# A two-layer hybrid backbone on one Trainium2 core: RWKV pair operands kept in DRAM between preparation and chain, and the state-space gate projected 256 columns at a time

## The chip, the cores and the metric

The kernel runs on one core of one Trainium2 chip. The metric is the device time of one execution in microseconds (us). The engines are TensorE (PE, with its weight loads as PEld), VectorE (DVE), ScalarE (ACT), GpSimd (POOL) and SyncE (SP), which issues nearly all DMAs. Before the change, three runs gave a median of 3539.37 us, from 3537.98 to 3549.52.

## The reference

Two layers over 512 tokens (256 context, 256 latent) of width 1024. A layer normalizes the tokens, projects them with one matrix `w_in`, and runs two branches on parts of the columns: an RWKV-7 branch (16 heads of 64, a delta-rule scan in both directions) and a state-space branch (8 groups of 4 heads, scans in both directions in chunks of 128). Both are gated, projected, summed and added to the stream; then a router sends each token to two of 32 experts. What the change touches is the RWKV scan and the gate of the state-space branch:

```python
def wkv7_scan(r, w, k, v, a, b, s0, reverse, emit):
    def step(S, inp):
        r_t, w_t, k_t, v_t, a_t, b_t = inp
        sa = jnp.einsum("bhij,bhj->bhi", S, a_t)
        S = S * w_t[:, :, None, :] + sa[..., None] * b_t[:, :, None, :] + v_t[..., None] * k_t[:, :, None, :]
        y = jnp.einsum("bhij,bhj->bhi", S, r_t) if emit else None
        return S, y
...
    y = y.reshape(bsz, -1, SSM_INNER) * jax.nn.silu(z.astype(F32))
    yg = y.reshape(bsz, -1, SSM_GROUPS, SSM_INNER // SSM_GROUPS)
    yg = yg * lax.rsqrt(jnp.mean(yg * yg, axis=-1, keepdims=True) + SSM_NORM_EPS)
```

`z` is the projection of the normalized tokens by 2048 columns of `w_in`, 256 for each group.

## The kernel before

**Stages.** A layer is one region. In the mixing stage the RWKV heads are worked in eight pairs of heads and the state-space branch in eight groups; then `merge` applies the branch projections, `route` the router, and the experts follow. Weights come as 512 KB pieces into `wst` (`load`, L760), ScalarE makes a half-precision high part `wh`, VectorE the low part `wl`, and each product is three matmuls.

**Order.** All calls of a layer are recorded first. `Recorder.schedule` (L519) then simulates the engines with costs per instruction and writes out one order for each engine, which the chip executes as it is. Each call belongs to a stream: `rw i` for pair i, `ssm i`, `gate i`, `mod n` and others; `mix_streams` (L1672) gives each stream a due time (96 us per pair and 99 us per group in layer 0, 100 and 105 us in layer 1). A tile has a tag; `SLOTS` (L209) says how many tiles of a tag may be held at once, and tiles of one tag are given out in the order of their streams' due times, unless `NEED` (L207) says otherwise. Streams whose name is `rw` or `sh` have weight and PSUM tags of their own (a leading `r`). SP's DMAs, stores and loads together, are in one such order too.

**One pair.** `rw_prep` (L1056) projects r, k and v, transposes v into SU, and calls `rw_dir` (L1152) for both directions, which makes the decays, the scaled operands X and Z, the transposed XT, and in matmuls `psg` the Gram matrices QA and AR. `rw_solve` (L1238) inverts sixteen unit-triangular 64x64 systems: QA goes through slB into slW, and 31 steps on VectorE, each a product slM and a sum into slY, give TT; `rw_merge` (L1287) joins the halves with QA. `rw_chain` (L1318) then forms `psat` (a transpose of Z's first half) and `psav` (QA times SU), multiplies both by TT (`psta`, `psua`), writes the first result over QA, and runs the seven dependent steps of the state (psH, St) and the outputs psY. `rw_out` (L1406) normalizes, adds bv, applies the gate and stores rwd. Z, SU, XT, QA, AR and TT have two slots each, one for each direction of one pair.

**One group.** `ssm_group` (L1474) projects x, B and C, convolves, and for each tile of 128 tokens (four in layer 0, two in layer 1) forms the scores and the outputs; the gate psz comes from two weight pieces z and u of 128 columns each, in 24 matmuls of 128 columns for each piece (L1570), with the tokens as the stationary operand:

```python
            for b in range(2):
                self.proj_t(pz[:, 128 * b:128 * b + 128], self.h, slice(128 * t, 128 * t + 128), Wz[b], 0, 128)
```

Of the kernel before, what the change touches and what calls it, by code (L numbers as in the profile page):

```python
# [12 lines left out]
F32 = mybir.dt.float32  # L13
F16 = mybir.dt.float16
BF16 = mybir.dt.bfloat16
# [6 lines left out]
NT = 512  # L22
# [52 lines left out]
def _unit_rows():  # L75

    h = (np.arange(128) // 16) % 2
    s = 2 * np.arange(16)[None, :] + h[:, None]
    return (s[:, :, None] == np.arange(32)).astype(np.float32)
# [27 lines left out]
_KDIM = {"in": 8, "rw": 8, "ssm0": 8, "ssm1": 8, "out0": 4, "out1": 4}  # L107
# [20 lines left out]
def pack(i):  # L128
# [7 lines left out]
    src = {"in": f["w_in"], "rw": f["w_branch_rw"], "ssm0": f["w_branch_ssm"][:, :1024],  # L136
# [72 lines left out]
SLOTS = {"R": 2, "sp": 2, "t5": 4, "y5": 3, "rt5": 5, "ot": 2, "z1": 4, "wst": 2, "wh": 2, "wl": 2, "rwst": 1, "rwh": 1, "rwl": 1, "r": 1,  # L209
# [3 lines left out]
CLASS = {"c4": 18, "c2": 40, "c1": 23, "ps": 8}  # L213
# [8 lines left out]
ENGINES = tuple(LAT)  # L222

# [34 lines left out]
class _Pool:  # L258
# [427 lines left out]
class Kernel:  # L686
# [10 lines left out]
    def setup(self):  # L697

        self.cp = self.pool("cp")
        self.dram = self.pool("dram", space=bass.MemoryType.DRAM)  # L700
        t = lambda n, s, d=F32: self.cp.tile(s, d, name=n)
        cst = self.cst = t("cst", [128, C_WA])
        self.c = lambda o, n=128: cst[:, o:o + n]
        self.ident = cst[:, C_ID:C_ID + 128]
        self.idb = t("idb", [128, 128], BF16)
        self.unit = t("unit", [128, 512], BF16)
        self.tri = t("tri", [128, 256], F16)
        self.io = t("io", [128, 256])
        self.iota, self.low = self.io[:, 0:128], self.io[:, 128:256]
# [12 lines left out]
        self.gd = self.dram.tile([128, 16, NT], F32, name="gd")  # L722
        self.ys = self.dram.tile([N_EXP * CAP[0], D], F32, name="ys")

    def constants(self):
# [4 lines left out]
        u = t([128, 512], F32, "unit32")  # L730
        nc.sync.dma_start(u, i["unit"].rearrange("p j t -> p (j t)"))
        nc.vector.tensor_copy(self.unit, u)
        nc.sync.dma_start(self.io, i["cst"][:, C_WS:C_T64F])
# [322 lines left out]
    def rw_prep(self, l, i):  # L1056
# [23 lines left out]
        vp = rp.tile([128, 64 + NT + 64], F32, name="v", bufs=2)  # L1080
        G.memset(vp[:, 0:64], 0.0)
        G.memset(vp[:, 64 + NT:], 0.0)
        v = S["v"] = vp[:, 64:64 + NT]
# [26 lines left out]
        for w0_ in (0, 4, 8):  # L1110
            pv = self.psum("t", [128, 4, 128], "psv")
            n = min(4, 9 - w0_)
            for w in range(n):
                T.transpose(pv[:, w], vp[:, 64 * (w0_ + w):64 * (w0_ + w) + 128], self.ident)
            if w0_ < 8:
                A.activation(SU[0][64:128, w0_:w0_ + 4, 0], pv[64:128, :, 0:64], AF.Copy)
            a = 0 if w0_ else 1
            A.activation(SU[0][0:64, w0_ + a - 1:w0_ + n - 1, 1], pv[0:64, a:n, 64:128], AF.Copy)
# [118 lines left out]

    def rw_solve(self, i):  # L1238
# [16 lines left out]
        G.tensor_copy(Y.rearrange("p j t -> p (j t)"), self.unit)  # L1255
# [62 lines left out]
    def rw_chain(self, l, i):  # L1318
# [14 lines left out]
        GT = wk.tile([128, 2, 8, 64], F32, name="GT", tag="slW")  # L1333
        St = wk.tile([128, 2, 8, 64], F32, name="St", tag="X")
        PH = []

        def batch(name, cs, out, lhs, rhs):

            ps = out or self.psum("g", [128, 8, 64], name)
            with nc.together():  # L1340
                for c in cs:
                    for e in E:
                        T.matmul(ps[rows[e], c], lhs(c, e), rhs(c, e), start=True, stop=True)
            return ps

        for d in range(2):
            SU = S["SU"][d]
            TT, XT, Z, AR = [S[x, d] for x in ("TT", "XT", "Z", "AR")]
            qa = S["QA", d].rearrange("p (c e) t -> p c e t", e=2)
            all8 = range(8)  # L1350
            mid = seq[d][1:7]

            ps = batch("psat", all8, None, lambda c, e: Z[rows[e], c, 0], lambda c, e: self.ident[rows[e], 64 * e:64 * e + 64])
            at = wk.tile([128, 8, 64], F32, name="at", tag="slY")
            A.activation(at, ps, AF.Copy)
            ps = batch("psav", all8, None, lambda c, e: qa[rows[1 - e], c, e], lambda c, e: SU[rows[1 - e], c, e])
            av = wk.tile([128, 8, 64], F32, name="av", tag="slB")
            V.tensor_copy(av, ps)
# [4 lines left out]
            ps = batch("psua", all8, None, lambda c, e: TT[rows[e], c], lambda c, e: av[rows[e], c])  # L1363
            A.activation(SU[rows[0], :, 0], ps[rows[0]], AF.Copy)
            V.tensor_copy(SU[rows[1], :, 1], ps[rows[1]])
            ps = batch("psgt", mid, None, lambda c, e: qa[rows[e], c, e], lambda c, e: XT[rows[e], c, 64 * e:64 * e + 64])
# [10 lines left out]
            ps = batch("psra", range(c0, 8), None, lambda c, e: qa[rows[e], c, e], lambda c, e: AR[rows[e], 2 * c + e])  # L1377
# [28 lines left out]
    def rw_out(self, l, i):  # L1406
# [12 lines left out]
        V.scalar_tensor_tensor(gw[64:96, 1], lo[64:96, 128:256], SW, gw[64:96, 1], op0=OP.mult, op1=OP.subtract)  # L1419
        y = wk.tile([128, NT], F32, tag="ot", name="gy", bufs=3)  # L1420
# [18 lines left out]
        G.tensor_tensor(y[:, :n], y[:, :n], S["bv"][:, :n], op=OP.add)  # L1439
# [34 lines left out]
    def ssm_group(self, l, g):  # L1474
# [59 lines left out]
        for t in range(t0, 4):  # L1534
# [34 lines left out]
            for b in range(2):  # L1569
                self.proj_t(pz[:, 128 * b:128 * b + 128], self.h, slice(128 * t, 128 * t + 128), Wz[b], 0, 128)  # L1570
# [101 lines left out]
    def mix_streams(self, l):  # L1672
# [50 lines left out]
    def route(self, l, X):  # L1723
# [63 lines left out]
        V.tensor_tensor(at, E1, E2, op=OP.add)  # L1787
        pp = self.psum("g", [128, nt, 32], "pspos")
        for t in range(nt):
            for u in range(t + 1):  # L1790
                T.matmul(pp[:, t], self.low if u == t else self.c(C_ONE), at[:, u], start=u == 0, stop=u == t)
# [391 lines left out]
```

## Time and profile before

| | us |
|---|---|
| median of three runs | 3539.37 |
| the profiled execution, its own time | 3538.96 |
| its span, first to last instruction | 3537.1 |
| TensorE busy | 3110.2 |
| VectorE busy | 2447.3 |
| ScalarE busy | 1705.4 |
| GpSimd busy | 769.3 |

The span divides into the head (to about 100 us), the mixing stage of layer 0 (to 1180), merge and router (to about 1400), the experts of layer 0 (to 1950), the mixing stage of layer 1 (2000 to 2905), its merge, and its experts. Busy times are shares of what an engine was occupied; for TensorE they hold the tails of matmuls that already run into one another, so that the distance between starts says more than a duration. In the views by tile, `first and last start` tell when the tile was worked on.

### The profile page before, as it was taken

How to read it: one execution, taken by the hardware profiler on the slowest of the kernel's cores; microseconds unless marked ns; L12 is line 12 of the kernel's file. 1: busy time of each engine (PE TensorE's matmuls, PEld its weight loads, DVE VectorE, ACT ScalarE, POOL GpSimd, SP SyncE). 2: the span in 40 equal slices, each digit the busy share in tenths (PEclk: the TensorE clock that was granted, in tenths of full speed). 3: DMA queues.
4: the chain of work that ended last, by engine and by line, in shares of the span. 5: the costliest groups of instructions: out<-in, count | busy, mean ns of one | idle time of the engine just before them, and what ended most of it. 6: DMA issues, size and time to landing. Idle time of an engine off the chain costs nothing. (4 is left out here: it accounts for less than half of the span.)

```text
span 3537.1 us, 86322 instructions
## 1 busy us (share of the span) xinstructions
PE 3110.2 (88%) x36050; PEld 2094.7 (59%) x36050; DVE 2447.3 (69%) x4491; ACT 1705.4 (48%) x3155; POOL 769.3 (22%) x1080
## 2 busy tenths in 40 slices
PE   7899889898998998999998778888889789899987
PEld 3566466475566457888886455666566668333332
DVE  4868868768778337999997788788988765221112
ACT  4554454454544325998886645554545434111111
POOL 1332332333232111111111133232333311000000
PEclk9999999999999997999999899999999889899998
DMA  7032231421312736999996411221212138999996
GB/s 283 28 106 73 93 118 51 151 100 43 120 57 98 276 104 222 412 401 397 396 394 249 154 63 45 74 69 50 75 61 71 53 125 299 346 399 398 399 398 243
DMA packets 241746, 662.65 MB, mean 187 GB/s; under 512 B 26688, under 2 KB 55104, under 8 KB 241344
## 3 DMA queue, kind: packets, MB, share of 16 engines
q1 hardware_dynamic: 236608, 640.22, 49.1%
q10 hardware_dynamic: 3584, 12.58, 0.9%
q8 instruction: 287, 4.70, 0.5%
q0 software_dynamic: 1152, 4.19, 0.3%
q14 instruction: 115, 0.94, 0.1%
HBM read 622.30 MB, written 34.60 MB: 186 GB/s over the span
## 5 line engine op out<-in xcount | busy, mean ns | idle before, releaser
L682 PE MATMUL mm<-h,wh 128*128 128x512 f16 (+1 forms) x2432 | 680.4, 363 | 11.0 <-ACT wh L682 11.0
L682 PEld LDWEIGHTS <-wh 128*128 128x128 f16 x3200 | 311.4, 99 | 280.7 <-issue 25.4
L682 PE MATMUL mm<-h,wl 128*128 128x512 f16 (+2 forms) x1216 | 439.0, 362 | 39.2 <-DVE wl L682 39.1
L682 DVE SCALAR_TENSOR_TENSOR ewl<-est,ewh 128x1024 f16<-128x1024 f32 x352 | 411.7, 1222 | 15.5 <-ACT ewh L682 12.4
L682 ACT ACTIVATE ewh<-est 128x1024 f16<-128x1024 f32 x384 | 382.6, 1049 | 32.4 <-PE pse L682 28.3
L682 DVE SCALAR_TENSOR_TENSOR wl<-wst,wh 128x1024 f16<-128x1024 f32 (+1 forms) x234 | 293.2, 1267 | 35.0 <-ACT wh L682 34.5
L682 PE MATMUL pse<-xg,ewh 128*128 128x96 f16 x4096 | 276.5, 206 | 2.9 <-DVE xg L682 0.8
L682 PEld LDWEIGHTS <-ewh 128*128 128x128 f16 x4096 | 265.8, 98 | 7.1
L682 PEld LDWEIGHTS <-wl 128*128 128x128 f16 (+1 forms) x1600 | 159.4, 100 | 181.4 <-DVE wl L682 47.9
L682 PE MATMUL pse<-xg,ewl 128*128 128x96 f16 x2048 | 264.0, 206 | 0.3 <-issue 0.2
L682 ACT ACTIVATE wh<-wst 128x1024 f16<-128x1024 f32 (+1 forms) x234 | 240.2, 1043 | 12.2 <-DMA wst<-in_wmix_dram 11.6
L682 PE MATMUL pse<-esh,xg 128*64 128x512 f32 x512 | 236.3, 597 | 0.0
L682 PE MATMUL pse<-est,xg 128*64 128x512 f32 x512 | 236.3, 597 | 0.0
L682 DVE SCALAR_TENSOR_TENSOR cva<-cvz,cwh,cva 128x512 f32<-128x512 f32 (+1 forms) x256 | 204.0, 797 | 0.4
L682 PEld LDWEIGHTS <-ewl 128*128 128x128 f16 x2048 | 199.4, 98 | 5.8 <-issue 4.1
L682 DVE TENSOR_TENSOR slM<-slY,slW 128x144 f32<-128x144 f32 (+22 forms) x496 | 175.0, 353 | 6.4
L682 POOL TENSOR_TENSOR ewl<-est,ewh 128x1024 f16<-128x1024 f32 x32 | 69.7, 2180 | 487.5 <-ACT ewh L682 414.6
L682 DVE SCALAR_TENSOR_TENSOR eyl<-psy,egs,eyh 128x512 f16<-128x512 f32 x32 | 24.0, 751 | 211.2 <-ACT eyh L682 211.2
L682 PEld LDWEIGHTS <-h 128*128 128x128 f16 x2496 | 150.0, 102 | 27.0 <-issue 21.1
L682 POOL TENSOR_TENSOR sht<-shz 128x512 f32<-128x512 f32 (+3 forms) x56 | 65.2, 1164 | 403.7 <-ACT shz L682 244.4
L682 PE MATMUL psz<-wh,h 128*128 128x128 f16 x1536 | 149.4, 225 | 0.0
L682 PE MATMUL psz<-wl,h 128*128 128x128 f16 x768 | 139.9, 225 | 8.3 <-DVE wl L682 8.3
(561 smaller groups left out, 7072.7 us busy)
## 6 DMA issues: line engine op xcount, KB each, us to landing
est<-in_w_dram SPq DMA_DIRECT2D x576, 512.0 KB, 7.5
wst<-in_wmix_dram SPq DMA_DIRECT2D x246, 512.0 KB, 4.7
esh<-in_w_dram SPq DMA_DIRECT2D x384, 256.0 KB, 6.6
wst<-in_wmod_dram SPq DMA_DIRECT2D x96, 512.0 KB, 6.0
ys<-ey ACTq DMA_DIRECT2D x32, 384.0 KB, 6.9
lot<-in_lora_dram SPq DMA_DIRECT2D x16, 256.0 KB, 4.8
gd<-gat SPq DMA_DIRECT2D x16, 256.0 KB, 2.0
smd<-smo SPq DMA_DIRECT2D x16, 256.0 KB, 3.4
```

The lines of the kernel that those rows point to most:

```text
L682: r = getattr(e, m)(*[real(x) for x in a], **{n: real(x) for n, x in k.items()})
```

## The change

Three things. **Pair operands in DRAM:** psat and psav move from the chain to the end of `rw_dir`, their results replace the first half of Z and the free half of SU; Z, SU, XT and AR are then stored to a DRAM tensor `sd`, and bv to another. The chain loads all four again into new tiles of the same tags; what it wrote over QA goes over Z, one copy of 128 rows by ScalarE in place of two of 64 rows by ScalarE and VectorE. Chain and output become a stream of their own, `ch i`, due 1 us after pair i+1's preparation and solve. GT gets a slot of its own. **The gate:** the pieces z and u are now the upper and the lower 512 rows of all 256 columns, and a tile's gate is 2 x 12 matmuls of 256 columns. **Constants:** the solve's start matrix Y is a memset by VectorE and a copy of 32 elements in place of a copy of 512; the zero borders of v go, with two half-width matmuls for the first and last block; the prefix-sum table `low` is loaded in `route`.

```diff
-        for n, o in (("x", X_ + 256 * i), ("y", X_ + 256 * i + 128), ("B", B_ + 128 * i), ("C", CC_ + 128 * i),
-                     ("z", Z_ + 256 * i), ("u", Z_ + 256 * i + 128)):
+        p += [(f"z{i}", "in0", r(Z_ + 256 * i, 256)), (f"u{i}", "in1", r(Z_ + 256 * i, 256))]
...
-SLOTS = {"R": 2, "sp": 2, "t5": 4, "y5": 3,
+SLOTS = {"GT": 1, "t5": 4, "y5": 3,
...
-CLASS = {"c4": 18, "c2": 40, "c1": 23, "ps": 8}
+CLASS = {"c4": 18, "c2": 41, "c1": 23, "ps": 8}
+LAG = 1
...
-            if tag in SPLIT and self.rec.stream[0] in ("rw", "sh"):
+            if tag in SPLIT and self.rec.stream[0] in ("rw", "sh", "ch"):
...
+        self.sd = self.dram.tile([128, 8, 2, 4, 1024], F32, name="sd")
+        self.sb_ = self.dram.tile([128, 8, NT], F32, name="sbv")
...
+        nc.sync.dma_start(self.sb_[:, i, :NT - o0], bv[:, :NT - o0])
         for d in range(2):
             self.rw_dir(l, i, d, S, kk, w0)
...
+        ps = self.batch("psat", lambda c, e: Z[rows[e], c, 0], lambda c, e: self.ident[rows[e], 64 * e:64 * e + 64])
+        A.activation(Z[:, :, 0], ps, AF.Copy)
+        ps = self.batch("psav", lambda c, e: QA[rows[1 - e], 2 * c + e], lambda c, e: SU[rows[1 - e], c, e])
+        A.activation(SU[rows[0], :, 0], ps[rows[0]], AF.Copy)
+        V.tensor_copy(SU[rows[1], :, 1], ps[rows[1]])
+        sd = self.sd[:, i, d]
+        nc.sync.dma_start(sd[:, 0], Z.rearrange("p c b t -> p (c b t)"))
+        nc.sync.dma_start(sd[:, 1], SU.rearrange("p c b t -> p (c b t)"))
+        nc.sync.dma_start(sd[:, 2], XT.rearrange("p c t -> p (c t)"))
+        if full:
+            nc.sync.dma_start(sd[:, 3], AR.rearrange("p c t -> p (c t)"))
+        else:
+            nc.sync.dma_start(sd[:, 3, 512:], AR[:, 8:].rearrange("p c t -> p (c t)"))
...
-        G.tensor_copy(Y.rearrange("p j t -> p (j t)"), self.unit)
+        V.memset(Y, 0.0)
+        G.tensor_copy(bass.AP(tensor=Y.tensor, offset=Y.offset, ap=[Y.ap[0], [34, 16], [1, 2]]),
+                      self.unit[:, None, :].to_broadcast([128, 16, 2]))
...
-            SU = S["SU"][d]
-            TT, XT, Z, AR = [S[x, d] for x in ("TT", "XT", "Z", "AR")]
+            TT = S["TT", d]
+            sd = self.sd[:, i, d]
+            Z = S["Z", d] = rp.tile([128, 8, 2, 64], F32, name="Z", bufs=4)
+            nc.sync.dma_start(Z.rearrange("p c b t -> p (c b t)"), sd[:, 0])
+            SU = rp.tile([128, 8, 2, 64], F32, name="SU", bufs=4)
+            nc.sync.dma_start(SU.rearrange("p c b t -> p (c b t)"), sd[:, 1])
+            XT = rp.tile([128, 8, 128], F32, name="XT", bufs=4)
+            nc.sync.dma_start(XT.rearrange("p c t -> p (c t)"), sd[:, 2])
+            AR = rp.tile([128, 16, 64], F32, name="AR", bufs=4)
+            nc.sync.dma_start(AR[:, 2 * c0:].rearrange("p c t -> p (c t)"), sd[:, 3, 128 * c0:])
-            ps = batch("psta", all8, None, lambda c, e: TT[rows[e], c], lambda c, e: at[rows[e], c])
-            A.activation(qa[rows[0], :, 0], ps[rows[0]], AF.Copy)
-            V.tensor_copy(qa[rows[1], :, 1], ps[rows[1]])
+            ps = batch("psta", lambda c, e: TT[rows[e], c], lambda c, e: Z[rows[e], c, 0])
+            A.activation(Z[:, :, 0], ps, AF.Copy)
...
+        bv = rp.tile([128, NT], F32, name="bv", bufs=2)
+        nc.sync.dma_start(bv[:, :n], self.sb_[:, i, :n])
...
-                self.proj_t(pz[:, 128 * b:128 * b + 128], self.h, slice(128 * t, 128 * t + 128), Wz[b], 0, 128)
+                self.proj_t(pz, lambda k: self.h(4 * b + k), tk, Wz[b], 0, 256, first=b == 0, last=b == 1)
...
             self.rw_solve(i)
+            rec.at(1, ("ch", i), h + 60e3 + P * (i + 1 + LAG) + 1e3)
             rec.tight = True
             self.rw_chain(l, i)
```

## Rows read from the trace of the kernel before

**Rows 1.** The page's slices: busy tenths of TensorE, VectorE, 88.4 us each.

```profile
PE   7899889898998998999998778888889789899987
...
DVE  4868868768778337999997788788988765221112
```

**Rows 2.** Stretches: length, PE, PEld, DVE, ACT, POOL busy, clock, DMA share, GB/s.

```profile
141.00:1075.00 934.00, 844.44 (x10330) 568.99 (x10328) 719.25 (x1475) 450.34 (x1008) 298.97 (x429) 0.96 0.27 93
2068.00:2822.00 754.00, 640.30 (x8138) 473.56 (x8137) 631.12 (x1336) 378.87 (x830) 251.62 (x412) 0.93 0.20 63
```

**Rows 3.** Tile slW, layers 0 and 1: count, ns min/median/max, first, last start.

```profile
L682 DVE STREAM_TRANSPOSE slW<-slB x8: 1924/1955/1974, 141.4 to 1074.5; 128x1024 f32<-128x1024 f32 x8
...
L682 DVE STREAM_TRANSPOSE slW<-slB x8: 1892/1936/1977, 2067.7 to 2821.5; 128x1024 f32<-128x1024 f32 x8
```

**Rows 4.** Stretches of one pair: solve, chain, prep; layer 0, then layer 1.

```profile
672.00:725.00 53.00, 45.30 (x287) 26.79 (x284) 50.90 (x114) 19.41 (x39) 14.07 (x25) 0.90 0.09 32
725.00:751.00 26.00, 24.14 (x688) 22.34 (x687) 14.14 (x31) 11.00 (x30) 4.72 (x6) 1.00 0.14 43
751.00:811.00 60.00, 53.24 (x510) 33.49 (x509) 41.25 (x70) 34.24 (x78) 25.07 (x32) 0.97 0.44 154
2277.00:2329.00 52.00, 43.15 (x274) 28.39 (x275) 48.36 (x113) 18.93 (x35) 15.40 (x24) 0.84 0.15 49
2329.00:2356.00 27.00, 24.86 (x654) 21.32 (x652) 20.61 (x43) 14.50 (x38) 3.21 (x7) 1.00 0.08 27
2356.00:2391.00 35.00, 26.58 (x249) 19.92 (x247) 25.29 (x42) 21.73 (x48) 16.31 (x30) 0.90 0.35 110
```

**Rows 5.** Tile Z of one pair: layer 0, then layer 1.

```profile
L682 PE MATMUL psg<-Z,X x64: 272/272/579, 792.3 to 807.6; 64*128 64x128 f32 x64
...
L682 PE MATMUL psY<-Z,St x56: 218/218/267, 751.4 to 753.0; 64*64 64x64 f32 x56
...
L682 PE MATMUL psat<-cst,Z x64: 218/218/267, 2329.7 to 2339.5; 64*64 64x64 f32 x64
...
L682 PE MATMUL psg<-Z,X x64: 272/272/579, 2372.9 to 2387.9; 64*128 64x128 f32 x64
...
L682 PE MATMUL psY<-Z,St x32: 218/218/267, 2356.5 to 2357.5; 64*64 64x64 f32 x32
```

**Rows 6.** DMA issues, us to landing; SP's waits from 141 to 1075.

```profile
wst<-in_wmix_dram SPq DMA_DIRECT2D x246, 512.0 KB, 4.7
...
smd<-smo SPq DMA_DIRECT2D x16, 256.0 KB, 3.4
...
xd<-xres SPq DMA_DIRECT2D x6, 512.0 KB, 3.0
...
SPq L682 <- PE psH L682: 231.4, 19, 58.7
```

**Rows 7.** Stretches: the fullest 100 us of the mixing stages.

```profile
300.00:400.00 100.00, 95.36 (x1361) 68.96 (x1360) 76.13 (x147) 54.50 (x130) 36.20 (x50) 1.00 0.32 104
```

**Rows 8.** Tile QA from 141 to 1075 us: the copy of psta.

```profile
L682 DVE COPY QA<-psta x14: 694/695/695, 200.8 to 1012.7; 64x512 f32<-64x512 f32 x14
```

**Rows 9.** Tile psz; its stretches; its weight loads; timeline of 512-column matmuls.

```profile
L682 PE MATMUL psz<-wh,h x32: 219/219/219, 161.2 to 163.8; 128*128 128x128 f16 x32
L682 PE MATMUL psz<-wl,h x16: 219/219/219, 161.2 to 163.8; 128*128 128x128 f16 x16
...
141.00:1075.00 934.00, 85.40 (x1344) 18.38 (x56) 0.96 0.27 93
2068.00:2822.00 754.00, 44.75 (x672) 9.43 (x28) 0.93 0.20 63
...
L682 PEld LDWEIGHTS <-h 128*128 128x128 f16 x2496 | 150.0, 102 | 27.0 <-issue 21.1
...
2289.00 0.38 PE L682 MATMUL mm<-h,wl 128*128 128x512 f16 x1
...
2290.94 0.38 PE L682 MATMUL mm<-h,wl 128*128 128x512 f16 x1
```

More of the change, by code (lines that the diff above doesn't have):

```diff
@@ L77, in _unit_rows @@
     h = (np.arange(128) // 16) % 2
-    s = 2 * np.arange(16)[None, :] + h[:, None]
-    return (s[:, :, None] == np.arange(32)).astype(np.float32)
+    return (h[:, None] == np.arange(2)).astype(np.float32)
 R_, WF_, WB_, K_, V_, AF_, AB_, G_ = 0, 1024, 1088, 1152, 2176, 3200, 3264, 3328
@@ L96, in _mix_pieces @@
     for i in range(8):
-        for n, o in (("x", X_ + 256 * i), ("y", X_ + 256 * i + 128), ("B", B_ + 128 * i), ("C", CC_ + 128 * i),
-                     ("z", Z_ + 256 * i), ("u", Z_ + 256 * i + 128)):
+        for n, o in (("x", X_ + 256 * i), ("y", X_ + 256 * i + 128), ("B", B_ + 128 * i), ("C", CC_ + 128 * i)):
             p.append((f"{n}{i}", "in", r(o, 128)))
+        p += [(f"z{i}", "in0", r(Z_ + 256 * i, 256)), (f"u{i}", "in1", r(Z_ + 256 * i, 256))]
     for j in range(8):
@@ L104, in _mix_pieces @@
     return p
-_KDIM = {"in": 8, "rw": 8, "ssm0": 8, "ssm1": 8, "out0": 4, "out1": 4}
+_KDIM = {"in": 8, "in0": 4, "in1": 4, "rw": 8, "ssm0": 8, "ssm1": 8, "out0": 4, "out1": 4}
 MIX = {}
@@ L135, in pack @@
     o["wmod"] = f["w_mod"].reshape(DEPTH, 8, 128, 3, 4, 2, 256).transpose(0, 3, 1, 5, 2, 4, 6)
-    src = {"in": f["w_in"], "rw": f["w_branch_rw"], "ssm0": f["w_branch_ssm"][:, :1024],
+    src = {"in": f["w_in"], "in0": f["w_in"][:, :512], "in1": f["w_in"][:, 512:], "rw": f["w_branch_rw"], "ssm0": f["w_branch_ssm"][:, :1024],
            "ssm1": f["w_branch_ssm"][:, 1024:], "out0": f["w_out"][:, :512], "out1": f["w_out"][:, 512:]}
@@ L208 @@
 SPLIT = {"wst", "wh", "wl", "mm", "t", "t5"}
-SLOTS = {"R": 2, "sp": 2, "t5": 4, "y5": 3, "rt5": 5, "ot": 2, "z1": 4, "wst": 2, "wh": 2, "wl": 2, "rwst": 1, "rwh": 1, "rwl": 1, "r": 1,
+SLOTS = {"GT": 1, "t5": 4, "y5": 3, "rt5": 5, "ot": 2, "z1": 4, "wst": 2, "wh": 2, "wl": 2, "rwst": 1, "rwh": 1, "rwl": 1, "r": 1,
          "k": 1, "v": 1, "kkt": 1, "bv": 1, "lot": 1, "lh": 1, "log": 1, "ll": 1, "gw": 1, "SU": 2, "Z": 2, "XT": 2, "QA": 2, "AR": 2, "TT": 2,
@@ L705, in setup @@
         self.idb = t("idb", [128, 128], BF16)
-        self.unit = t("unit", [128, 512], BF16)
+        self.unit = t("unit", [128, 2])
         self.tri = t("tri", [128, 256], F16)
-        self.io = t("io", [128, 256])
-        self.iota, self.low = self.io[:, 0:128], self.io[:, 128:256]
+        self.iota = t("iota", [128, 128])
         self.id2 = t("id2", [128, 64])
@@ L729, in constants @@
         nc.vector.tensor_tensor(self.id2, self.ident[:, 0:64], self.ident[:, 64:128], op=OP.add)
[L730 to L733, printed above, removed]
+        nc.sync.dma_start(self.unit, i["unit"])
+        nc.sync.dma_start(self.iota, i["cst"][:, C_IOTA:C_IOTA + 128])
         u = t([128, 256], F32, "tri32")
@@ L1079, in rw_prep @@
         k = S["k"] = rp.tile([128, NT], F32, name="k", bufs=2)
[L1080 to L1083, printed above, removed]
+        v = S["v"] = rp.tile([128, NT], F32, name="v", bufs=2)
         ps = self.psum("mm", [128, NT])
@@ L1109, in rw_prep @@
         S["SU"] = SU
-        for w0_ in (0, 4, 8):
+        for w0_ in (0, 4):
             pv = self.psum("t", [128, 4, 128], "psv")
[L1112 to L1116, printed above, removed]
+            with nc.together():
+                for w in range(4):
+                    if w + w0_:
+                        T.transpose(pv[:, w], v[:, 64 * (w0_ + w) - 64:64 * (w0_ + w) + 64], self.ident)
+            if not w0_:
+                with nc.together():
+                    T.matmul(pv[64:128, 0], v[:, 0:64], self.ident, start=True, stop=True)
+                    T.matmul(pv[0:64, 0], v[:, NT - 64:NT], self.ident, start=True, stop=True)
+                A.activation(SU[0][0:64, 7, 1], pv[0:64, 0, 64:128], AF.Copy)
+            A.activation(SU[0][64:128, w0_:w0_ + 4, 0], pv[64:128, :, 0:64], AF.Copy)
             a = 0 if w0_ else 1
-            A.activation(SU[0][0:64, w0_ + a - 1:w0_ + n - 1, 1], pv[0:64, a:n, 64:128], AF.Copy)
+            A.activation(SU[0][0:64, w0_ + a - 1:w0_ + 3, 1], pv[0:64, a:4, 64:128], AF.Copy)
         G.tensor_copy(SU[1][64:128, :, 0], SU[0][64:128, :, 0])
@@ L1236, in rw_dir, with batch @@
                                     mi[:, None, :].to_broadcast([128, 4, 64]), op=OP.mult)
+        rows = self.rows2
+        SU = S["SU"][d]
+        ps = self.batch("psat", lambda c, e: Z[rows[e], c, 0], lambda c, e: self.ident[rows[e], 64 * e:64 * e + 64])
[11 more added lines that the diff above has]
+            nc.sync.dma_start(sd[:, 3, 512:], AR[:, 8:].rearrange("p c t -> p (c t)"))
+    rows2 = (slice(0, 64), slice(64, 128))
+    def batch(self, name, lhs, rhs, cs=range(8)):
+        ps = self.psum("g", [128, 8, 64], name)
+        with self.nc.together():
+            for c in cs:
+                for e in range(2):
+                    self.nc.tensor.matmul(ps[self.rows2[e], c], lhs(c, e), rhs(c, e), start=True, stop=True)
+        return ps
     def rw_solve(self, i):
@@ L1332, in rw_chain @@
         yo = lambda c, e: py[rows[e], 64 * c - o0:64 * c - o0 + 64]
-        GT = wk.tile([128, 2, 8, 64], F32, name="GT", tag="slW")
+        GT = wk.tile([128, 2, 8, 64], F32, name="GT")
         St = wk.tile([128, 2, 8, 64], F32, name="St", tag="X")
         PH = []
[L1337 to L1344, printed above, removed]
@@ L1346, in rw_chain @@
-        for d in range(2):
-            SU = S["SU"][d]
-            TT, XT, Z, AR = [S[x, d] for x in ("TT", "XT", "Z", "AR")]
-            qa = S["QA", d].rearrange("p (c e) t -> p c e t", e=2)
-            all8 = range(8)
-            mid = seq[d][1:7]
[L1353 to L1358, printed above, removed]
-            ps = batch("psta", all8, None, lambda c, e: TT[rows[e], c], lambda c, e: at[rows[e], c])
-            A.activation(qa[rows[0], :, 0], ps[rows[0]], AF.Copy)
-            V.tensor_copy(qa[rows[1], :, 1], ps[rows[1]])
-            ps = batch("psua", all8, None, lambda c, e: TT[rows[e], c], lambda c, e: av[rows[e], c])
+        batch = self.batch
@@ new lines, in rw_chain @@
+        for d in range(2):
+            TT = S["TT", d]
[8 more added lines that the diff above has]
+            nc.sync.dma_start(AR[:, 2 * c0:].rearrange("p c t -> p (c t)"), sd[:, 3, 128 * c0:])
+            mid = seq[d][1:7]
+            ps = batch("psta", lambda c, e: TT[rows[e], c], lambda c, e: Z[rows[e], c, 0])
+            A.activation(Z[:, :, 0], ps, AF.Copy)
+            ps = batch("psua", lambda c, e: TT[rows[e], c], lambda c, e: SU[rows[e], c, e])
@@ L1364, in rw_chain @@
             A.activation(SU[rows[0], :, 0], ps[rows[0]], AF.Copy)
             V.tensor_copy(SU[rows[1], :, 1], ps[rows[1]])
-            ps = batch("psgt", mid, None, lambda c, e: qa[rows[e], c, e], lambda c, e: XT[rows[e], c, 64 * e:64 * e + 64])
+            ps = batch("psgt", lambda c, e: Z[rows[e], c, 0], lambda c, e: XT[rows[e], c, 64 * e:64 * e + 64], mid)
             for cs in ((slice(0, 3), slice(5, 8)) if d else (slice(1, 7),)):
@@ L1376, in rw_chain @@
                                  skip_group_check=True)
-            ps = batch("psra", range(c0, 8), None, lambda c, e: qa[rows[e], c, e], lambda c, e: AR[rows[e], 2 * c + e])
+            ps = batch("psra", lambda c, e: Z[rows[e], c, 0], lambda c, e: AR[rows[e], 2 * c + e], range(c0, 8))
             V.tensor_tensor(Z[:, c0:, 1], Z[:, c0:, 1], ps[:, c0:], op=OP.add)
@@ L1438, in rw_out @@
         A.activation(y[:, :n], y[:, :n], AF.Identity, scale=self.pv("lnw", 1, i), bias=self.pv("lnb", 1, i))
-        G.tensor_tensor(y[:, :n], y[:, :n], S["bv"][:, :n], op=OP.add)
+        G.tensor_tensor(y[:, :n], y[:, :n], bv[:, :n], op=OP.add)
         pg = self.psum("t", [128, NT], "psgate")
@@ L1787, in route @@
         V.tensor_tensor(at, E1, E2, op=OP.add)
+        low = self.tile([128, 128], F32, "low")
+        nc.sync.dma_start(low, self.i["cst"][:, C_LOW:C_LOW + 128])
         pp = self.psum("g", [128, nt, 32], "pspos")
@@ L1790, in route @@
             for u in range(t + 1):
-                T.matmul(pp[:, t], self.low if u == t else self.c(C_ONE), at[:, u], start=u == 0, stop=u == t)
+                T.matmul(pp[:, t], low if u == t else self.c(C_ONE), at[:, u], start=u == 0, stop=u == t)
         pos = tl("pos")
```

## The prediction

> **What bounds the kernel now.** I read the slices first: between the head and the expert stages lie two mixing stages (100 to 1180 us and 2000 to 2905 us, slices 2 to 13 and 24 to 32) in which TensorE's digits go from 7 to 9 and VectorE's from 6 to 9 [rows 1]. The experts' stages contain nothing that the change touches, so the question is what sets the pace of the mixing stages. The busy time over seven periods of the RWKV pairs says that no engine does: TensorE is busy 844.4 of 934 us in layer 0 and 640.3 of 754 us in layer 1, VectorE 719.3 and 631.1 us, and the DMA engines 0.27 and 0.20 of the time [rows 2]. The pairs themselves keep a strict beat: the first wide transpose of the solve (slW) comes eight times between 141.4 and 1074.5 us, and eight times between 2067.7 and 2821.5 us, which is 133.3 and 107.7 us per pair [rows 3]. The table by phase of one pair shows why [rows 4]. During the solve (52 to 53 us) VectorE is busy 0.93 to 0.96 of the time and TensorE 0.83 to 0.85; during merge and chain (26 to 27 us) it is the reverse, TensorE 0.92 to 0.93, VectorE 0.54 to 0.76; in the rest (60 us in layer 0, 35 us in layer 1), the next pair's preparation, TensorE has 0.89 and 0.76. So the three phases run one after another, each full on one engine only. The operands that hold them apart are visible by their times: the last matmul of the chain that reads Z is at 2357.5 us, and the next pair's first Gram matmul with its own Z comes at 2372.9, its last at 2387.9; in layer 0 it is 753.0, then 792.3 to 807.6 [rows 5]. Z, SU, XT, QA and AR have two buffers each (one per direction), so pair i+1 can't have its operands before the chain of pair i is done.
>
> **The change part by part.**
>
> *Parking and the lag.* Prep now ends with the transposes psat and psav, and Z, SU, XT and AR go to DRAM; their buffers come free before the solve instead of after the chain. QA stays in SBUF, but its last reader is now the merge. The chain of pair i, which reloads the four tiles, ranks behind the prep of pair i+1, and so falls beside the solve of pair i+1. The ring chain-prep-solve falls into two shorter rings:
> - Buffers: chain from the last psat on (2339.5 to 2357.5, 18 us), prep up to the last Gram matmul (807.6-751.4 = 56 us in layer 0, 2387.9-2356.5 = 31 us in layer 1 [rows 5]), psat and psav with their copies at most 10 us (with the merge they lie between 2329 and 2339.5), a store and a reload at 3.0 and 4.7 us to landing [rows 6] about 8 us: 92 and 67 us.
> - QA: solve 52 us, merge at most 10 (the same stretch), the two Gram rounds 15 (2372.9 to 2387.9), the transposes before the solve 3 (to 2391): 80 us.
>
> Both are shorter than 133.3 and 107.7 us, so the engines set the pace next. How full can they get? I take 0.94, between the 0.93 of the chains [rows 4] and the best 100 us of the stage, 95.4 [rows 7]. Layer 0: 844.4/0.94 = 898 instead of 934, gain 36 us (VectorE would allow 765). Layer 1: 640.3/0.94 = 681 instead of 754, gain 73 us (VectorE, 623/0.94 = 662, is close behind). First prep and last chain have no partner before or after, so I count seven periods of eight. Ends: at 0.98, 72 and 101 us; at half the effect, 55 us together.
>
> *Its own cost.* psat and psav are the same 128 matmuls each; they now run beside the solve's first steps, which don't wait for them. Per pair VectorE loses two copies of 0.694 us (psta now goes through ScalarE alone) [rows 8] and gains a memset of Y of 512 elements (not in the trace; between 0.1 us and that copy's 0.7; I take 0.2, since it reads nothing): 1.2 us less, which is the 623 above. ScalarE gains two such copies and is idle for half of the stage [rows 2]. POOL's copy of Y shrinks; its cover is the same solve start. Nine transposes of v become seven and two half-width matmuls: no difference. SP issues 18 DMAs more per pair, eight stores and eight loads of 512 KB (the AR ones half in layer 1) and bv twice: 8.4 MB and 7.3 MB. The DMA engines moved 93 GB/s at 0.27 busy, so 344 GB/s when full [rows 2]: 24 us more of DMA time per pair beside the 36 that it has now, in a period of 125. That is no bound. SP, however, is one queue in order: it waited 231 us for the chain's psH in layer 0, once 58.7 us [rows 6]. A store of a parked tile waits for ScalarE or VectorE, a reload for a free buffer, and behind both stand the weight loads, which have three buffers. I cost it at nothing, because a weight piece feeds about 5 us of matmuls and two more are loaded by then; without that cover it is the second rival.
>
> *The gate (psz).* 2304 matmuls of 128 columns become 1152 of 256. The columns are the same. 48 of them start between 161.2 and 163.8 us, one each 56 ns; nine of 512 columns take 1.94 us, 216 ns each, so 256 columns take 108 [rows 9]. The sum at this rate goes from 129 to 124 us. Over both layers TensorE is busy 130 us for 2016 of them, 65 ns each [rows 9], part of it tails and low clock: at most 24 us. I take 6. The Trainium skill, page "TensorE: Matmul & The Clock Gate", section "Back-to-back issue gap", gives about 81 ns for a sustained pair of weight load and 128-column matmul and 131 ns for 512; by that the edit would save an estimated 36 us or more. The rows disagree at both widths, and I go by them.
>
> *Rest.* The smaller unit constant saves a little in the head, the table for the router's prefix sum is now loaded in the router's stage, ahead of its use: nothing either way, at worst 2 x 4.7 us of landing.
>
> **Sum.** The profiled execution took 3538.96 us, 0.4 us under the median of the runs. 3539-36-73-6 = 3424; I say 3425.
>
> **The rivals.**
> 1. *The solve stays the bound.* VectorE is already 0.93 to 0.96 full there; its chain of small dependent instructions is stretched by every instruction of the chain that now comes between. If in layer 1 VectorE's idle time of 17.6 us per period ((754-631)/7) falls only to 14, and layer 0 gains 2 us a period, it is 7 x 5.6 = 39 us: 3500 (between 3490 and 3539). For it: the full solve phase. Against it: layer 0 has 31 us of idle VectorE per period.
> 2. *SP's queue (slower).* Stores that wait for their producers hold back weight loads, and TensorE starves. It decides from 115/14 = 8.2 us of starving per pair; at 12 us it is 168-115 = 53 us: 3592. For it: the long waits of SP [rows 6]. Against it: with those waits TensorE is still 0.90 busy in layer 0.
> 3. *Slow DRAM pieces (slower).* Each parked tile is 128 pieces of 4 KB, 256 KB apart. The 256 KB of smd, also spread, took 3.4 us, half a weight piece 2.4 [rows 6]. It decides at four times the time of contiguous pieces: 96 + 36 = 132 us of DMA in a period that was 133. At 4.25 times layer 0 needs 138 us and layer 1 (21 us of parking, 22 of its own) 112: 7 x 4.7 + 7 x 4.3 = 63 us more than now, less 6: 3596. Against it: smd is 1.4 times, not four. The Trainium skill, page "DMA: Bandwidth & Descriptors", section "Latency and other measured facts", says that large powers of two as the pitch of rows cost bandwidth, 207 GB/s at 512 KB and 103 at 4 MB. No run here shows it yet.
> 4. *Weight loads bound psz after all.* If each pair cost its weight load's 102 ns [rows 9], 2304 would take 235 us and half as many 124: 111 instead of 6, so 3320. The 56 ns speak against it. It is the rule of the page on TensorE named above, at its hardest.
>
> **How the numbers follow.** Forecast 0.62 (3340 to 3490), rivals 0.18, 0.12, 0.04, 0.04. About 0.3%, 11 us, is what a measurement of this kernel can tell from no change. The first rival gives 0.12 faster and 0.06 same; slower are the second and third: 0.78, 0.06, 0.16. The range 3320 to 3530 holds the forecast with its ends and most of the first rival, and leaves out the slower ones.
>
> **What would show it.** The chain's psta and psua should start while slM of the next pair runs; slW should beat every 120 to 128 and 95 to 100 us; TensorE's busy share should be near 0.94 in both layers; psz should take 108 ns per matmul. Longer solves (over 60 us) at the same beat speak for the first rival; TensorE waiting for wh or wl behind SP for the second; landings of the parked tiles over 15 us for the third. I am wrong if the beat falls and the time does not, or if it stays at 133 and 108 us.

## The result and the profile after

The changed kernel takes 3479.13 us (median of four, 3478.76 to 3486.93), the kernel before 3541.14 us in the same comparison: a ratio of 0.9827 [0.9804, 0.9849], 62 us or 1.7 % faster. I had forecast 3425 us. The execution that was profiled is the slowest of the four, 3486.93 us; its span is 3484.8 us, 52.3 us under that of before.

Tile slW of the changed kernel, layers 0 and 1, answers to [rows 3] (count, ns, first and last start):

```profile
L683 DVE STREAM_TRANSPOSE slW<-slB x8: 1908/1953/1970, 153.1 to 1039.3; 128x1024 f32<-128x1024 f32 x8
...
L683 DVE STREAM_TRANSPOSE slW<-slB x8: 1889/1944/1967, 2041.9 to 2772.1; 128x1024 f32<-128x1024 f32 x8
```

The beat is 126.6 and 104.3 us, 6.7 and 3.4 us shorter. In layer 0 that makes 47 us over seven periods, yet the layer ends only 22.7 us earlier: its first slW comes 11.7 us later, and the last one's distance to the end of the merge grew by 11 us. The stretches of those seven periods in each layer (columns of [rows 2]):

```profile
153.10:1039.30 886.20, 815.30 (x9180) 530.82 (x9177) 696.20 (x1439) 447.75 (x1005) 286.32 (x405) 0.97 0.46 164
2041.90:2772.10 730.20, 632.84 (x7471) 458.85 (x7471) 605.30 (x1306) 376.57 (x821) 246.54 (x389) 0.92 0.39 134
```

TensorE is busy 0.92 and 0.87 of them, against 0.90 and 0.85 before. It does 29 us less in layer 0's periods than in [rows 2]. Half of that work now stands ahead of the first slW, the other half in the tail behind the last one. The head up to the first slW, before (first) and after (second):

```profile
0.00:141.40 141.40, 106.72 (x779) 58.53 (x780) 86.75 (x165) 74.95 (x155) 30.16 (x51) 0.94 0.50 186
```

```profile
0.00:153.10 153.10, 121.45 (x957) 65.32 (x957) 92.94 (x175) 84.27 (x166) 35.61 (x57) 0.89 0.49 188
```

The tail, from just behind the last slW to the end of the merge's matmuls, before (first) and after (second):

```profile
1076.80:1305.20 228.40, 213.69 (x1798) 119.92 (x1797) 120.62 (x215) 73.29 (x123) 30.30 (x39) 0.96 0.45 157
```

```profile
1041.80:1281.20 239.40, 228.50 (x1972) 128.32 (x1973) 128.13 (x230) 78.69 (x135) 36.29 (x42) 0.96 0.53 185
```

TensorE fills this tail to 0.95 and has 15 us more work there, as it has in the head. One pair in three stretches as in [rows 4], but now solve, rest of the preparation, Gram rounds, since the previous pair's chain lies beside the solve; layer 0, then layer 1:

```profile
508.00:556.00 48.00, 45.01 (x739) 28.95 (x736) 44.70 (x113) 23.51 (x46) 9.44 (x17) 1.00 0.45 163
556.00:622.00 66.00, 62.65 (x529) 39.40 (x518) 43.69 (x73) 38.66 (x96) 26.72 (x34) 1.00 0.49 180
622.00:637.30 15.30, 14.83 (x198) 10.00 (x196) 13.48 (x30) 6.43 (x12) 4.44 (x11) 1.00 0.90 336
...
2336.00:2384.00 48.00, 43.92 (x649) 29.43 (x646) 46.00 (x118) 24.58 (x51) 10.24 (x21) 1.00 0.31 107
2384.00:2418.70 34.70, 33.47 (x289) 25.85 (x289) 28.63 (x51) 22.15 (x53) 18.83 (x28) 0.90 0.38 126
2418.70:2443.50 24.80, 17.90 (x307) 14.64 (x306) 18.65 (x34) 9.28 (x20) 6.84 (x11) 0.79 0.68 256
```

During the solves TensorE's share rose from 0.85 and 0.83 to 0.94 and 0.92: much of the chain moved there, as meant. The chain's psta against the steps slM of the solve, one pair of layer 1, before (first) and after (second):

```profile
L682 PE MATMUL psta<-at,TT x64: 218/218/267, 2337.0 to 2342.4; 64*64 64x64 f32 x64
...
L682 DVE TENSOR_TENSOR slM<-slY,slW x31: 155/318/1004, 2280.0 to 2328.2; 128x144 f32<-128x144 f32 x3, 128x4 f32<-128x4 f32 x2, 128x16 f32<-128x16 f32 x2, 128x36 f32<-128x36 f32 x2
```

```profile
L683 PE MATMUL psta<-Z,TT x64: 218/218/267, 2335.4 to 2357.6; 64*64 64x64 f32 x64
...
L683 DVE TENSOR_TENSOR slM<-slY,slW x31: 149/318/467, 2338.9 to 2377.6; 128x144 f32<-128x144 f32 x3, 128x4 f32<-128x4 f32 x2, 128x16 f32<-128x16 f32 x2, 128x36 f32<-128x36 f32 x2
```

Before, psta came after the last step of its own pair's solve. Now its first direction starts just ahead of the next pair's steps, its second among them. Layer 0's pair is 0.95 full over its period. Layer 1 has a hole in the Gram rounds: 0.72, at a clock of 0.79 (part of it at 1.2 GHz), with the DMA engines at 0.68. What TensorE waited for in layer 1's periods (us in total, times, longest):

```profile
PE psta L683 <- DMA Z<-sd: 17.4, 8, 3.8
PE pscw L683 <- ACT lp L683: 11.8, 5, 4.5
PE psW L683 <- DVE slO L683: 8.1, 5, 2.3
PE psua L683 <- DMA SU<-sd: 6.3, 4, 1.9
```

The first and the fourth are reloads of parked tiles. Landings of these, and of a weight piece of the same size, from the table of DMA issues (KB, median us):

```profile
wst<-in_wmix_dram SPq DMA_DIRECT2D x246, 512.0 KB, 6.3
...
sd<-XT SPq DMA_DIRECT2D x32, 512.0 KB, 3.6
sd<-Z SPq DMA_DIRECT2D x32, 512.0 KB, 4.0
sd<-SU SPq DMA_DIRECT2D x32, 512.0 KB, 4.9
XT<-sd SPq DMA_DIRECT2D x32, 512.0 KB, 5.6
Z<-sd SPq DMA_DIRECT2D x32, 512.0 KB, 6.2
SU<-sd SPq DMA_DIRECT2D x32, 512.0 KB, 7.2
```

### The profile page after: what moved, and what is told of

Its sections match the earlier page's. It is cut to its first block, busy times and chain, and to the rows that moved or that the text cites. A ratio compares the mean times of both kernels' runs of the same rounds, so it can differ in the third digit from the quotient of the medians.

```text
span 3484.8 us, 84587 instructions
## 1 busy us (share of the span) xinstructions
PE 3117.4 (89%) x34930; PEld 2072.5 (59%) x34930; DVE 2418.7 (69%) x4474; ACT 1725.3 (50%) x3189; POOL 773.3 (22%) x1048
## 5 line engine op out<-in xcount | busy, mean ns | idle before, releaser
L683 DVE TENSOR_TENSOR slM<-slY,slW 128x144 f32<-128x144 f32 (+22 forms) x496 | 162.7, 328 | 8.3
L683 ACT ACTIVATE eu<-pse 128x384 f32<-128x384 f32 (+1 forms) x64 | 34.5, 540 | 243.4 <-PE pse L683 243.4
L683 DVE TENSOR_REDUCE slY<-slM 128x2 f32<-128x4 f32 (+23 forms) x496 | 147.3, 297 | 7.2
L683 PE MATMUL psz<-wh,h 128*128 128x256 f16 x768 | 150.3, 283 | 0.0
```

What stands on the lines that cost most here:

```text
L683: r = getattr(e, m)(*[real(x) for x in a], **{n: real(x) for n, x in k.items()})
```

## The experiments

All times in one table; layer 0 is counted to the end of the last `ey` in the profiled execution, layer 1 is the rest of its span, and the beat is the mean distance of slW. The ratio is to the kernel before, from runs of the same session; that kernel's median was 3541 us beside the change and 3544 to 3546 in the later sessions, so differences to the changed kernel, which are of medians, are good to some 5 us.

| kernel | median us | ratio [95 %] | layer 0, 1 (us) | beat 0, 1 (us) |
|---|---|---|---|---|
| before | 3541.1 | 1 | 1930.6, 1606.5 | 133.3, 107.7 |
| changed | 3479.1 | 0.9827 [0.9804, 0.9849] | 1907.9, 1576.9 | 126.6, 104.3 |
| e1 parking only | 3486.6 | 0.9838 [0.9825, 0.9852] | 1922.6, 1563.5 | 129.9, 101.0 |
| e2 gate only | 3505.9 | 0.9891 [0.9874, 0.9909] | 1916.2, 1590.6 | 130.7, 105.7 |
| e3 no lag | 3535.6 | 0.9981 [0.9971, 0.9991] | 1948.6, 1585.5 | 136.3, 105.5 |
| e4 last chain due earlier | 3481.0 | 0.9822 [0.9809, 0.9835] | 1905.0, 1576.9 | 127.5, 103.9 |
| e5 gate in the old order | 3541.1 | 0.9986 [0.9975, 0.9997] | 1933.9, 1610.2 | 133.8, 107.7 |
| e6 reloads reckoned at 4.0 us | 3462.8 | 0.9764 [0.9748, 0.9780] | 1899.4, 1570.3 | 126.4, 101.5 |
| e7 half solve, before | 3433.7 | 0.9685 [0.9669, 0.9702] | 1875.4, 1556.4 | 126.3, 102.0 |
| e8 half solve, changed | 3451.2 | 0.9733 [0.9717, 0.9748] | 1907.1, 1543.3 | 129.6, 100.0 |
| e9 e6 and e4 | 3448.5 | 0.9729 [0.9715, 0.9744] | 1896.1, 1559.5 | 126.1, 101.6 |
| e10 e1 and e6 | 3484.1 | 0.9833 [0.9818, 0.9848] | 1914.7, 1567.5 | 128.1, 101.6 |
| e11 a copy before each reload | 3608.2 | 1.0177 [1.0159, 1.0194] | 1984.9, 1625.5 | 137.9, 110.3 |
| e12 another order | 3477.2 | 0.9811 [0.9788, 0.9835] | 1893.3, 1585.9 | 125.0, 104.1 |

### Which part brings it: e1 to e4

e1 puts back the six 128-column pieces and the old gate loop; e2 is the kernel before with the other side of that diff:

```diff
-                self.proj_t(pz[:, 128 * b:128 * b + 128], self.h, slice(128 * t, 128 * t + 128), Wz[b], 0, 128)
+                self.proj_t(pz, lambda k: self.h(4 * b + k), tk, Wz[b], 0, 256, first=b == 0, last=b == 1)
```

> The change with its gate part undone: z and u are projected 128 columns at a time from the old packing, the parking stays. Theory A (the parking brings the gain, by splitting the ring of a pair): 3476 to 3490 us, since the 24 gate matmuls of a tile take 109 ns each after the change where 48 took 54 ns each before; beats of slW 126 and 104 us as in the changed kernel. Rival B (the gate brings a good part): 3500 us or more, with the beats nearer to 133 and 108 us.

> The kernel before with the new gate alone, nothing parked. Theory A: 3533 to 3545 us, no change that can be measured, beats of slW 133 and 108 us. Rival B (the gate brings a good part of the 62 us): 3520 us or less.

The parking alone takes 58 us off, the gate alone 38, both together 62. e1's time came as theory A says, though not its beats, 129.9 and 101.0 us where I expected 126 and 104. e2 didn't: a part that I had put at 6 us brought 38, and the two don't add.

e3 sets `LAG = 0`; e4 changes one due time:

```diff
-            rec.at(1, ("ch", i), h + 60e3 + P * (i + 1 + LAG) + 1e3)
+            rec.at(1, ("ch", i), h + 60e3 + P * (i + 1 + LAG * (i < 7)) + 1e3)
```

> The changed kernel with the due time of each pair's chain one period earlier (LAG 0), so that parked operands come back as soon as the solve is done. Theory A (what counts is that the buffers are free, the chain may run early): 3480 to 3500 us, with the beats of slW within 2 us of 126 and 104. Rival C (what counts is that the chain is allowed to run late and fill the solve of the next pair): 3515 to 3545 us, nearly all of the gain gone, with beats near 133 and 108 us.

> The changed kernel with the last pair's chain alone due one period earlier. In the changed kernel the stretch from the last slW of layer 0 to the end of the branch took 241.9 us where it took 230.7 before, and the last chain's St took 40 us of it. Theory D (the late due time starves the last chain, and the merge waits for it): 3455 to 3470 us, 10 to 25 us less than the changed kernel, with the tail of layer 0 back under 231 us. Rival E (TensorE is busy there with work that has to be done anyway): 3473 to 3485 us, the tail unchanged in sum.

e3 is rival C: with the chain due in its own pair's period, parking and gate together give 7 us (0.9981 of 3544), less than the gate alone. That is 56 us above the changed kernel, more than an order alone moves anything below (33 us). So it isn't the empty buffers that pay but the permission to run the chain a period late, beside the next solve. The lag also lengthens the head: e3 has its first slW at 139.6 us, the changed kernel at 153.1. e4 is rival E: the last chain of layer 0 is done 33 us earlier (its last St starts at 1111.7 instead of 1145.1 us), yet the merge ends only 1.6 us earlier. In that tail TensorE is full of work that has to be done anyway, which is what the two tail rows above show.

### Why the gate alone brings 38 us: e5

The matmuls are 256 wide, but recorded and priced as two of 128, and merged only when the order is written out:

```diff
+                        for c in (0, 128):
+                            nc.tensor.matmul(pz[:, c:c + 128], zx, Wz[b][w][:, k, c:c + 128], **f)
+                        nc.wide[len(nc.ops) - 2] = [("matmul", (pz, zx, Wz[b][w][:, k, 0:256]), f)]
+                        nc.wide[len(nc.ops) - 1] = []
...
-                for m, a, k in o.calls:
+                for m, a, k in self.wide.get(i, o.calls):
```

> The kernel before with the gate's matmuls 256 columns wide from the new packing, but everything put in order as if they were still 128 wide, so that each engine's order is that of the kernel before with two narrow matmuls replaced by one wide one. The gate alone took 38 us off where nothing was expected of it. Theory F (the narrower count of matmuls changes the order in which the list scheduler puts all engines' work, and the gain is that order, with fewer matmuls falling into half clock): 3530 to 3545 us. Rival G (the width itself saves TensorE time): 3500 to 3515 us, as the gate alone with its own order.

Theory F. In the old order the wide gate is worth 5 us (0.9986 of 3546; the interval gives 1 to 9). The other 33 us belong to the order that the scheduler happened to write: ScalarE's 3155 instructions come in the same order in the traces of e5 and of the kernel before, and in another one in e2. One way in which an order pays is visible: the same matmuls, in the seven periods of each layer, e5 first, then e2:

```profile
141.20:1077.00 935.80, 845.05 (x9652) 557.33 (x9650) 718.04 (x1472) 449.94 (x1007) 300.21 (x429) 0.96 0.27 92
2070.90:2825.00 754.10, 637.60 (x7802) 464.16 (x7801) 630.97 (x1337) 378.35 (x830) 251.54 (x412) 0.93 0.20 63
```

```profile
141.90:1056.80 914.90, 834.47 (x9653) 549.13 (x9651) 710.92 (x1473) 449.33 (x1007) 297.61 (x429) 0.98 0.28 94
2054.40:2794.20 739.80, 625.96 (x7799) 452.75 (x7798) 621.45 (x1334) 377.06 (x830) 254.25 (x412) 0.95 0.20 64
```

An equal number of matmuls (within 3) occupies TensorE 10.6 and 11.6 us less, at a granted clock that is 0.02 higher: less of it fell to 1.2 GHz. The stretches are 21 and 14 us shorter, so the clock goes with about two thirds of it; whether it causes the shorter stretch or follows from fewer pauses isn't settled by these rows.

The gate's own matmuls run as forecast. One gate of the changed kernel, 24 matmuls of 256 columns:

```profile
L683 PE MATMUL psz<-wh,h x16: 272/273/273, 2398.1 to 2400.6; 128*128 128x256 f16 x16
L683 PE MATMUL psz<-wl,h x8: 272/273/273, 2398.2 to 2400.5; 128*128 128x256 f16 x8
```

### Is the solve still the bound: e7 and e8

`for t in range(16, 32)` becomes `range(16, 17)`: steps 17 to 31 of the solve are left out, in the kernel before and in the changed one.

> The kernel before with steps 17 to 31 of the solve left out, so 30 of its 62 VectorE instructions per pair are gone and its last inverse rows are not computed. Theory A (the ring prep, solve, chain sets the pace before the change): each layer falls until TensorE's 0.94 is the bound, 35 us in layer 0 and 70 us in layer 1, so 3420 to 3470 us. Rival (the ring is not the bound): 3525 us or more.

> The changed kernel with steps 17 to 31 of the solve left out, as in the run before this one. Theory A (parking has taken the solve off the path): 0 to 20 us less than the changed kernel, 3459 to 3479 us. Rival 1 of the prediction (the solve still bounds through the buffers that it holds or through VectorE): 40 us less or more, 3439 us or less, as much as the same cut saves in the kernel before.

The cut saves 112 us before the change (0.9685 of 3546), as theory A says, though by layer it is 55 and 50 us and not 35 and 70. After it, 28 us, between theory A and rival 1, and by layer it is both: layer 0 is the same within 1 us (1907.1 for 1907.9), layer 1 falls by 34 us (1543.3 for 1576.9). Of these, 16 us lie below every order here with the whole solve (the best is e9's 1559.5). The seven periods with half a solve, kernel before first, then changed:

```profile
141.90:1026.00 884.10, 832.29 (x10336) 566.65 (x10336) 649.91 (x1265) 454.01 (x1015) 300.92 (x429) 0.98 0.28 98
2012.50:2726.60 714.10, 630.41 (x8115) 471.10 (x8114) 558.48 (x1123) 379.71 (x828) 249.73 (x412) 0.94 0.21 66
```

```profile
149.20:1056.60 907.40, 828.99 (x9211) 540.53 (x9207) 644.16 (x1232) 444.98 (x1006) 287.56 (x409) 0.95 0.45 161
2041.40:2741.30 699.90, 613.20 (x7489) 446.47 (x7489) 547.91 (x1099) 375.10 (x821) 250.67 (x395) 0.94 0.41 141
```

Without parking and with half a solve TensorE reaches 0.941 in layer 0, the 0.94 that I had taken, but only 0.883 in layer 1; with both it is 0.876 there. And once the solve is short, the changed kernel is the slower of the two, 3451 for 3434 us: parking with the new gate then costs 17 us. All of it and more lies in layer 0, which takes 1907.1 us with parking and 1875.4 without.

### What the reloads cost: e6, e9, e10, e11, e12

e6 gives the scheduler a truer landing time for the reloads, e10 the same on e1, e9 e6 with the diff of e4:

```diff
         o.lat = 900 if o.bytes and eng == "scalar" else 1500 if o.bytes and eng != "sync" else LAT[eng]
+        if o.bytes and eng == "sync" and reads[0].tensor.name.startswith("sd"):
+            o.lat = 4000
```

> The changed kernel with the scheduler told that a reload of a parked tile lands 4.0 us after its transfer instead of 0.9 us, so that reloads are issued earlier or their readers put later; nothing else is changed. In the changed kernel TensorE waits 17.4 us for Z and 6.3 us for SU in the beats of layer 1, 3.8 and 6.1 us in layer 0. Theory H (these waits and what queues behind them are why layer 1 gained 24 us and not 73): the waits fall under 5 us in each layer and the time is 3450 to 3470 us. Rival I (the waits only move to the next operand, since DVE and POOL feed the pair's preparation no sooner): 3473 to 3490 us with the reload waits gone.

> The changed kernel with reloads reckoned at 4.0 us, as in the run that took 3463 us, and the last pair's chain due one period earlier, as in the run that changed nothing alone. If the last chain is held only by late reloads and late dues together: 3445 to 3458 us. If TensorE has that work to do in any order: 3459 to 3467 us, as with the reloads alone.

> The parking with the old, narrow gate, and reloads reckoned at 4.0 us: the same edit as in the run that took 3463 us, on the order of the run that took 3487 us. Theory H (late reloads cost about 16 us in whatever order): 3465 to 3478 us, TensorE's waits for reloaded tiles under 5 us in the beats of each layer. Theory F alone (those 16 us were another order by chance): 3480 to 3495 us or more.

e6 takes 3462.8 us and its waits for parked tiles are gone; e9 takes 3448.5, the fastest that I have with all of the computation, 2.7 % under the kernel before. But e10, where the waits fell as well (in layer 1 from 6.4 and 3.4 us to 0.2 and none for Z and SU), only goes from 3486.6 to 3484.1 us. That is theory F's figure. But e1 had only 18 us of such waits in both layers' periods, the changed kernel 34, so e10 had less to win. e12 asks how far an order moves by itself:

```diff
-            return c * w / 2.4 + 3, col, 0
+            return c * w / 2.4 + 4, col, 0
```

> The changed kernel with the scheduler's price of every matmul raised by 1 ns and nothing else: the same work, put in another order for no reason of its own. It sizes what an order by chance is worth. Theory H for the 3463 us run (16 us from the reloads reckoned at 4.0 us) stands only if this run stays within 8 us of the changed kernel, 3471 to 3487 us; if it is off by 10 us or more in either direction (theory F), those 16 us can't be put down to the reloads, and the same holds for the difference between two orders anywhere here.

The total stays within 2 us, so by the line as written theory H stands for e6; but layer 0 is 15 us shorter and layer 1 9 us longer, so single layers move by an order alone as far as e6 gained in each (8.5 and 6.6 us). What removing the waits is worth is therefore open, between 2 us (e10) and 16 us (e6). e9 falls into its first range. Of its 14 us over e6, 11 stand in layer 1, where the tail from the last slW to the end of the merge takes 162.9 us in e6, 151.2 in e9 and 152.7 in the changed kernel: it gives back what e6's order had lost there.

e11 asks from the other side, at a fixed order, by a copy that nothing waits for:

```diff
                 for m, a, k in o.calls:
+                    if m == "dma_start" and a[1].tensor.name.startswith("sd"):
+                        e.dma_start(self.echo(a[1]), a[1])
```

> The changed kernel with a copy of the same tile from DRAM to spare DRAM issued on SP ahead of every reload, every engine's order otherwise as it was: 128 transfers more, none of which anything waits for, so every reload starts and lands later. Theory H (late reloads stop TensorE): its waits for Z and SU in the beats of layer 1 rise from 24 us to 40 us or more, and the time is 3490 to 3520 us. Rival J (the parked transfers are covered by other work, as the prediction took them): 3474 to 3486 us.

It costs 129 us (3608.2 for 3479.1): the direction of theory H, but three times its upper end of 41 us, and far from rival J. In the table of DMA issues the reloads of Z and SU now land 2 us later than above (so do their stores, 6.0 and 7.3 us):

```profile
Z<-sd SPq DMA_DIRECT2D x32, 512.0 KB, 8.2
SU<-sd SPq DMA_DIRECT2D x32, 512.0 KB, 9.3
```

TensorE's waits for them in layer 0's periods (first) and layer 1's (second):

```profile
PE psua L685 <- DMA SU<-sd: 30.3, 11, 6.9
PE psta L685 <- DMA Z<-sd: 29.9, 10, 5.6
```

```profile
PE psta L685 <- DMA Z<-sd: 39.7, 11, 6.6
PE psua L685 <- DMA SU<-sd: 15.2, 7, 3.6
```

The seven periods in each layer:

```profile
150.30:1115.60 965.30, 849.84 (x9183) 553.78 (x9185) 695.18 (x1440) 446.44 (x1005) 286.49 (x405) 0.93 0.50 179
2119.50:2891.40 771.90, 645.12 (x7473) 468.19 (x7473) 606.34 (x1307) 375.76 (x821) 245.38 (x389) 0.90 0.45 158
```

In layer 1 those waits grew by 31 us, in layer 0 from 10 to 60 us; the layers grew by 49 and 77 us, their periods by 42 and 79. Most of the rest of the periods is TensorE's own busy time: nearly the same matmuls (within 3) take 12 and 35 us more, at a granted clock of 0.90 and 0.93 instead of 0.92 and 0.97. Weight pieces held up behind the copies are not the reason, since the waits of mm for wl fell (2.2 to 0.8 us, 2.5 to 2.2). So parked transfers that land 2 us later lengthen the beat by 6 us (layer 1) to 11 us (layer 0), which is what transfers on a ring would do. Parked tiles have two slots: a slot is stored by pair i+1, then reloaded for pair i, then must be read before pair i+2 can write it. On such a ring every microsecond of landing counts, several times per pair. That this is the way in which the 129 us arise is argued from the code and the waits, since SP's 128 more issues were not tried without their traffic.

## Why the prediction was right, and where it was off

- **The beat and the phases**: right for the kernel before and for the way of the gain. The chain from psta's second direction on runs beside the next solve, the first direction's psta just ahead of it, and TensorE's share in the solve went to 0.94 and 0.92; e7 shows that the solve held the kernel before, and e3 that without the lag 7 us are left. That the engines take over as pacemaker isn't shown. In layer 0 the solve no longer counts, since e8's cut is worth nothing there; but e7, which parks nothing, does that layer in 32 us less than e8 with the same products, so TensorE's work isn't what bounds e8. By e11 the reloads are a suspect, but e6, with no wait for them left, takes only 8.5 us off that layer: this stays open.
- **Layer 0, 36 us**: the periods gained 47, the layer 23. The step that failed is "seven periods of eight", with head and tail taken as they were: the late chain moves work out of the periods to the ends, and where TensorE is 0.95 full that work costs its own time (15 us in the tail's rows, and 15 us more ahead of the first slW). The periods' own share was 0.92 where I took 0.94.
- **Layer 1, 73 us**: this is the main miss. Its periods gained 24 us (754 to 730) and the layer 30 with all its other stages. The step that failed is "How full can they get? I take 0.94": the 0.95 of [rows 7] is a stretch of layer 0, and layer 1's own preparation stood at 0.76 in [rows 4]. No version here passes 0.883 in layer 1's periods, not even with half a solve and nothing parked. At the 0.867 that was measured, the 640.3 us of before make 739, a gain of 15; the rest is that the periods hold 7.5 us less of TensorE's work. The first rival named the reason in part: half a solve still gives 34 us in this layer, 16 of them clear of order, so VectorE's solve is still on its path. By that rival's own measure, VectorE's idle time per period there, nothing was won: 17.8 us ((730.2-605.3)/7) after 17.6. The periods shrank by 24 us while 26 us of VectorE's work left them. But its sign, solves over 60 us, did not come: they take 48 us in both layers' rows, 52 to 53 before. The prediction had the solve as a rival for both layers, and it was true of one.
- **The ring of QA, 80 us**: too short. It let the whole preparation but the Gram rounds run beside the solve. In the rows of one pair, merge to next solve still takes 59 us in layer 1 (2384.0 to 2443.5), and VectorE, 0.96 full in the solve, writes the next pair's Z only from 2417.6 us on. That VectorE's load is the reason is argued, not shown.
- **DMA and SP, cost nothing**: half right. TensorE's waits for weights didn't grow (mm for wl went from 23.7 to 2.2 us in layer 1, from 12.1 to 2.5 in layer 0), so the second rival is out. Landings of 3.6 to 7.2 us put the third out: a weight piece, contiguous in DRAM, takes 6.3 us here, so the pitch of 256 KB shows no cost. But a reload took 5.6 to 7.2 us where I had 4.7, stood in front of psta and psua, and by e11 lies on the path. My buffer ring had room for it on paper, 67 us in a period of 97. The memset of Y, for which I took 0.2 us, takes 0.485; over seven periods that is 2 us of VectorE.
- **The gate, 6 us**: right for its own work, 5 us by e5. At 24 matmuls with starts from 2398.1 to 2400.6 us, one starts every 109 ns, the forecast 108. The fourth rival, and the rule of the Trainium skill's page "TensorE: Matmul & The Clock Gate" (section "Back-to-back issue gap") on which it leaned, are not borne out: its 36 us or more would have to show in the old order too, and there is 5. What I had no term for is that any edit makes the scheduler write another order: 33 us for the gate alone, nothing that can be told from noise when parking is there as well (3479 for e1's 3487).
- **The sum**: 114 us forecast, 62 measured. 3479 lies inside the forecast's own band (3340 to 3490), near its upper end, and below the first rival's (3490 to 3539). Where it lies there is in part luck: the step from the phases to 0.94 failed in both layers, and the order alone, for which there was no term, moves this kernel by up to 33 us. That parking pays does hold over orders: the seven kernels here that park, lag and do the whole solve, without e11's copies, lie between 3448 and 3487 us, the ones that park nothing at 3506 and 3541. How much it pays doesn't hold: anything from 19 to 93 us.

## What to carry to other kernels

How full an engine can get is read from the stage in question: a best stretch of another stage is no bound for it. Work that is moved out of a steady beat is still to be done at the ends, so count the whole stage, not the periods. Where a list scheduler rewrites the order after every edit, hold the order fixed for one run before a part's gain is put down to the part.

## What was not expected

The order alone, with the same instructions, moved this kernel by 33 us (e5 against e2), of which TensorE's own busy time makes 22 us, at a clock of 0.98 and 0.95 instead of 0.96 and 0.93. A transfer that nothing waits for, put ahead of each reload, cost 129 us for 128 of them while the DMA engines stood at 0.50 of their time in those periods of layer 0: a low mean share of the DMA engines says little about a transfer that two slots depend on.
